# The last expert group of a mixture of experts summed in PSUM over all columns, and the combination that follows it reordered

## The chip, the cores and the metric

The kernel runs on one core of a Trainium2 chip. The metric is the device time of one execution in microseconds (us). Times of the kernel before are 2087.3, 2087.61 and 2090.02 us; their median is 2087.61 us.

## The reference, cut to what matters

The program is two transformer blocks on 512 tokens of D = 1024 columns. The first ends with a mixture of experts, the second begins with a normalisation and a product with a wide matrix:

```python
def expert_block(acc, blk):                 # blocks of rows sorted by expert
    tok, wts, e = blk
    out = swiglu(h_pad[tok], w_gu[e], w_down[e])
    return acc.at[tok].add(out * wts[:, None].astype(out.dtype)), None
...
f = acc[:N] + swiglu(h, w_sh_gu, w_sh_down)             # routed sum + shared expert
x = x_lat + gt2 * rms_norm(f, g_post_ffn)               # end of the first block
...
xn = rmsnorm(x, norm_mix_gain)                          # start of the second block
...                                                     # xn @ w_in, of which w_v is the first part used
```

So every token's row needs the sum of eight routed expert outputs and of one shared expert, two normalisations one after the other, and only then can the next product start.

## The kernel before, in words

Tokens lie in four tiles of 128 (NT = 4). All products are made in three passes: each factor is split into a rounded high part (ACT, L133 for weights, L153 for activations) and a low rest (DVE, L134 and L154), and TensorE adds hi·hi, lo·hi and hi·lo (`mm3`, L147 to L149).

**Expert groups.** Routed rows are worked off in groups of blocks. For a group, the loop in the function around L1297 to L1350 makes the expert's output rows `ey` (ACT, L1072), in a ring of three tiles. Columns 0 to 383 (CA = 384) of `ey` are split into `eys` hi (ACT, L1085) and lo (GpSimd, L1086), and TensorE adds them to the tokens' sums `acc[t]` in PSUM through a one-hot matrix `eoh` (`expert_add`, L1095). Columns 384 to 1023 go by an indirect DMA of GpSimd's software queue (`expert_send`, L1076) which adds them in DRAM, in two buffers `cb[0]` and `cb[1]`. The last group has one block of 96 rows.

**Shared expert.** After the groups comes a branch for overflow blocks, not taken here (L1356); all engines meet at it. Then `shared_out` adds the shared expert's product: per token tile six matmuls of 512 columns into `acc[t]` (columns 0 to 511), six into `mm` (columns 512 to 1023).

**Combination** (`second_block`, L1462 to L1535). SP loads, per token tile, the DRAM sums `cf<-cb` (L1462) and `cg<-cb` (L1463), and the rows `g`, `cx`, `gmix`. `take(t)` forms the whole sum in `cf`: ACT copies `acc`'s 384 columns (L1480), DVE (tile 0) or GpSimd (tiles 1 to 3) adds `cg` (L1481), DVE adds `acc`'s other 128 columns (L1482) and `mm` (L1483) straight from PSUM. ACT takes the sum of squares (L1486); `rstd` (L178 to L186) is eight small DVE operations for one tile, or eleven for tiles 1 to 3 at once. Then the product with the gain and the add to `cx` (tile 0: L714; later tiles `norm`: L1510 and the `add2` L1404, 640 columns on DVE, 384 on GpSimd), the second sum of squares (ACT, L1486 or L1388), a second `rstd`, and `xn` (L1498 or L1390). TensorE transposes `xn` (`tp`, L1398), ACT and DVE split the transposed tile into `x` hi and lo (L153, L154), and the product with w_v begins: two halves of 512 columns per tile, (0,0), (0,1), (1,0) and so on, 24 matmuls each, `tp` of the next tile after them or between them. w_v comes in four pieces of two units: v0 and v1 feed the first halves, v2 and v3 the second; v3's low parts are made by GpSimd (L134).

PSUM of the first block is given back by `release()`; only then can the second block's PSUM tiles (the transposes first of all) be used. The order on DVE, ACT and GpSimd inside the combination is the order in which it is written; TensorE's and SP's is set by a scheduler. The combination's tiles lie in SBUF that the expert part's tiles had used, so its first writers wait for the last readers of those.

Of the kernel before, what the change touches and what calls it, by code (L numbers as in the profile page):

```python
# [11 lines left out]
F = mybir.dt.float32  # L12
R = mybir.dt.float32r
# [3 lines left out]
AF = mybir.ActivationFunctionType  # L17
OP = mybir.AluOpType
# [6 lines left out]
D = 1024  # L25
# [41 lines left out]
class Kernel:  # L67
# [1009 lines left out]
                                          in_=y[p0:p1, CA:], in_offset=None, bounds_check=T - 1, oob_is_err=False,  # L1077
                                          compute_op=OP.add)

    def expert_parts(self, mp, y, row):  # L1080

        nc = self.nc
        m = row.shape[0]
        yh, yl = (mp.tile([128, CA], R, tag=f"eys{i}", name="eys", bufs=2)[0:m] for i in range(2))
        nc.scalar.activation(yh, y[0:m, :CA], AF.Copy)  # L1085
        last = nc.gpsimd.tensor_sub(yl, y[0:m, :CA], yh.bitcast(F))  # L1086
        oh = mp.tile([128, T], R, tag="eoh", name="eoh", bufs=2)[0:m]
        nc.vector.tensor_scalar(oh, self.route["iota"][0:m], row, None, op0=OP.is_equal)
        return (oh, (yh, yl)), last
# [7 lines left out]
    def shared_expert(self, mp, pp, gp, gT, h2T):  # L1097
# [4 lines left out]
        for h in range(2):  # L1102
            hs = slice(h * H, (h + 1) * H)
            sg = []
            for u in range(2):
                for j in range(2):
# [7 lines left out]
                        nc.vector.tensor_mul(sg[j], sg[j], ps[:, :H])  # L1114
                        self.split_ps(gT[0][:, j, hs], gT[1][:, j, hs], sg[j])
                    yield
    def shared_out(self, ps, gT, w, t, half):

        c = slice(half * 512, (half + 1) * 512)
        for i in range(2):  # L1120
            self.mm3(ps, [z[:, i, t * 128:(t + 1) * 128] for z in gT], [z[:, i, c] for z in w],
                     half == 1 and i == 0, i == 1)

    def first_block(self):

# [84 lines left out]
    def experts(self, mp, pp, h2d, cb, acc, shared, gT, sums, grow, ahead, extra):  # L1210
# [83 lines left out]
        nc.vector.tensor_scalar(zr, r["iota"], -1.0, None, op0=OP.is_equal)  # L1294
        for t in range(NT):
            nc.tensor.matmul(acc[t], zr[:, 0:128], zr, start=True, stop=False)
        late, sums = None, []  # L1297
        for g in range(len(groups) + 1):
            turn(g + 1)
            outs, now, y = [], None, []  # L1300

            def advance():

                if late:
                    lg, a, nums = late
                    aT = [self.expert_turn(more, pp, x) for x in a]
                    y.extend(mp.tile([128, D], F, tag="ey", name="ey", bufs=3) for _ in a)
                    for j, e in enumerate(nums):
                        outs.append((e, [(b, aT[b], tabs[rows_of[lg][b]][1], y[b], p0, p1)
                                         for b, parts in enumerate(groups[lg][1]) for i, p0, p1, _ in parts if i == j]))  # L1310

            def add():
                while sums:
                    self.expert_add(acc, *sums.pop(0))

            def finish():

                if not outs:
                    return
                e, parts = outs.pop(0)  # L1320
                lg = late[0]
                self.expert_out(pp, dn(e), [p[1:] for p in parts])
                last = None
                if not outs:
                    add()
                    for b, i in enumerate(rows_of[lg]):
                        s, last = self.expert_parts(mp, y[b], tabs[i][0])
                        sums.append(s)
                with tc.issue_after(last.ins) if last else ExitStack():
                    for b, _, _, y_, p0, p1 in parts:  # L1330
                        i = rows_of[lg][b]
                        gi = tabs[i][3][[p[1] for p in groups[lg][1][b]].index(p0)]
                        self.expert_send(y_, gi, p0, p1, next(sent))

            if g < len(groups):
                es, bs = groups[g]
                a = [mp.tile([128, 256], F, tag="eact", name="act", bufs=4)[0:b[-1][2]] for b in bs]
                now = g, a, []
                for j, e in enumerate(es):
                    e = number(e)  # L1340
                    now[2].append(e)
                    self.expert_in(mp, pp, gu(e), [(xT[g][b][i], a[b], p0, p1) for b, parts in enumerate(bs)
                                                   for i, (k, p0, p1, _) in enumerate(parts) if k == j],
                                   None if j else advance)
                    finish()
            else:
                advance()
            while outs:
                finish()
            late = now  # L1350
# [20 lines left out]

        rest = []
        for t in range(NT):
            self.shared_out(acc[t], gT, w, t, 0)
            rest.append(pp.tile([128, 512], F, tag="mm", name="mm", bufs=4))
            self.shared_out(rest[t], gT, w, t, 1)
        return rest


# [13 lines left out]
    def turn_tile(self, pp, xn, hi, lo, t):  # L1393
        ts = slice(t * 128, (t + 1) * 128)
        for u in range(2):
# [1 line left out]
            for i in range(4):  # L1397
                self.nc.tensor.transpose(ps[:, i], xn[:, (4 * u + i) * 128:(4 * u + i + 1) * 128], self.ident)  # L1398
            self.split_ps(hi[:, 4 * u:4 * u + 4, ts], lo[:, 4 * u:4 * u + 4, ts], ps)

    def add2(self, dst, a, b):

        for sl, e in ((slice(0, ADD_COLS), self.nc.vector), (slice(ADD_COLS, D), self.nc.gpsimd)):
            e.tensor_add(dst[:, sl], a[:, sl], b[:, sl])  # L1404

    def quarters(self, name, *at):

# [33 lines left out]
    def second_block(self, x1d, cb, acc, more, release):  # L1441
# [9 lines left out]
        vr = vctx.enter_context(right("b2v")).tile([128, NT, D], F, name="rv")  # L1451
        with right("comb") as wp, ExitStack() as wctx:
            fs = [wp.tile([128, D], F, name=f"cf{t}") for t in range(NT)]
            f2 = [wp.tile([128, D - CA], F, name=f"cg{t}") for t in range(NT)]

            sq, y = vr[:, 3], vr[:, 2]
            g3 = wp.tile([128, D], F, name="g3")
# [1 line left out]
            ss = wp.tile([128, NT], F, name="css")  # L1459
            rows = [slice(t * 128, (t + 1) * 128) for t in range(NT)]  # L1460
            def sums(t):
                nc.sync.dma_start(fs[t][:, CA:], cb[0][rows[t], :])  # L1462
                nc.sync.dma_start(f2[t], cb[1][rows[t], :])  # L1463

            sums(0)
# [4 lines left out]
                sums(t)  # L1470
            for t in range(1, NT):
                nc.sync.dma_start(x1[t], x1d[rows[t], :])
            units = self.each_unit(wctx, self.quarters("w_v_2"), self.first_raws, [None, None, None, nc.gpsimd])
            ET = mybir.EngineType
            with tc.manual_schedule(engines={ET.DVE, ET.Activation, ET.Pool}):
                w = [next(units), next(units)]

                def take(t):

                    nc.scalar.activation(fs[t][:, 0:CA], acc[t][:, 0:CA], AF.Copy)  # L1480
                    (nc.gpsimd if t else nc.vector).tensor_add(fs[t][:, CA:], fs[t][:, CA:], f2[t])  # L1481
                    nc.vector.tensor_add(fs[t][:, CA:512], fs[t][:, CA:512], acc[t][:, CA:])  # L1482
                    nc.vector.tensor_add(fs[t][:, 512:], fs[t][:, 512:], more[t])  # L1483

                def squares(x, ss):
                    nc.scalar.activation(sq, x, AF.Square, accum_out=ss)  # L1486


                take(0)
                squares(fs[0], ss[:, 0:1])  # L1490
                nc.vector.tensor_mul(y, fs[0], g3)
                self.scale_add(x1[0], y, self.rstd(wp, ss[:, 0:1], D), x1[0])
                ss0 = wp.tile([128, 1], F, name="css0")
                squares(x1[0], ss0)
                nc.vector.tensor_mul(y, x1[0], gain)
                take(1)
                xn = wp.tile([128, D], F, tag="xn", name="xn", bufs=2)
                nc.vector.tensor_scalar(xn, y, self.rstd(wp, ss0, D), None, op0=OP.mult)  # L1498
                for t in range(2, NT):
                    take(t)  # L1500
                for t in range(1, NT):
                    squares(fs[t], ss[:, t:t + 1])
                release()
                pp = ctx.enter_context(tc.tile_pool(name="b2ps", bufs=1, space=PSUM))
                rs = self.rstd(wp, ss[:, 1:], D)
                self.turn_tile(pp, xn, xs[0], xs[1], 0)
                nc.sync.dma_start(xd[rows[0], :], x1[0])

                def norm(t):
                    nc.vector.scalar_tensor_tensor(fs[t], fs[t], rs[:, t - 1:t], g3, op0=OP.mult, op1=OP.mult)  # L1510
                    self.add2(x1[t], x1[t], fs[t])
                    nc.sync.dma_start(xd[rows[t], :], x1[t])

                def product(t, half, between=None):
                    ps = self.tile_gemm(pp, self.columns(xs), w, half, t, between)
                    nc.scalar.activation(vr[:, t, half * 512:(half + 1) * 512], ps, AF.Copy)

                norm(1)
                w.append(next(units))
                xn = self.normed_tile(wp, x1[1], gain)  # L1520
                w.append(next(units))
                w = [w[:2], w[2:]]
                for t in range(NT):
                    product(t, 0)
                    if t + 2 < NT:
                        norm(t + 2)
                    turn = None
                    if t + 1 < NT:
                        turn = lambda: self.turn_tile(pp, xn, xs[0], xs[1], t + 1)
                    product(t, 1, turn)  # L1530
                    if t + 2 < NT:
                        xn = self.normed_tile(wp, x1[t + 2], gain)
# [409 lines left out]
RAW2 = 2  # L1942
MOD_SPLIT = (1, 2, 3)
RAW3 = 2
ADD_COLS = 640

CA = 384
AHEAD = 3
# [139 lines left out]
```

## Time and profile before

| | |
|---|---|
| runs | 2087.3, 2087.61, 2090.02 us; median 2087.61 us |
| the profiled execution's own time | 2089.45 us |
| its span on the core | 2087.7 us, so 1.75 us lie around the span |
| mean granted TensorE clock | 0.982 of full speed |
| TensorE busy | 1969.7 us (94% of the span) |
| DVE, ACT, GpSimd busy | 1524.8, 1156.2, 512.1 us |

The places that matter lie between 1255 and 1335 us after the span's start. PE is TensorE, DVE VectorE, ACT ScalarE, POOL GpSimd, SP the engine that issues most loads. A line number is one of the kernel before; where the changed kernel's own line is meant, the text says so.

### The profile page before, as it was taken

The numbers are of one execution on the slowest core, as the hardware profiler recorded it, in microseconds if no ns is written. First come the engines' busy times: TensorE is split into PE (matmuls) and PEld (weight loads), VectorE is DVE, ScalarE is ACT, GpSimd is POOL, SyncE is SP. The second block draws the span as 40 slices with busy tenths as digits, with TensorE's granted clock in tenths as the row PEclk, the third lists the DMA queues.
The fourth block names the chain that finished last, engine by engine and source line by source line (L and its number), as shares of the span: only waits on it lengthen the run. The fifth ranks groups of instructions, "written<-read, shape, count | busy, mean of one in ns | idle before, by whom it ended". The sixth has DMA issues, their size and how long they took to land. (4 is left out here: it accounts for less than half of the span.)

```text
span 2087.7 us, 27579 instructions
## 1 busy us (share of the span) xinstructions
PE 1969.7 (94%) x9935; PEld 1583.8 (76%) x9935; DVE 1524.8 (73%) x2689; ACT 1156.2 (55%) x1734; POOL 512.1 (25%) x291
## 2 busy tenths in 40 slices
PE   7999999999889999899999996999999999999997
PEld 4877888787877677667766775777788888888886
DVE  6667766657899899899999997456863345755657
ACT  6544433233368798788888885334232324554554
POOL 0322221101236465445634323111100000000000
PEclk9999999999899999999999998999999999999999
DMA  7201126543489999899998997411122234546553
GB/s 294 80 22 43 68 98 252 212 166 132 168 302 349 312 343 351 284 353 340 353 347 306 330 333 252 143 61 61 41 91 91 99 143 134 159 126 197 123 140 81
DMA packets 73167, 406.03 MB, mean 194 GB/s; under 512 B 11758, under 2 KB 12735, under 8 KB 31428
## 3 DMA queue, kind: packets, MB, share of 16 engines
q1 hardware_dynamic: 58084, 360.18, 46.7%
q0 software_dynamic: 14944, 44.06, 9.7%
q8 instruction: 79, 1.29, 0.2%
q14 instruction: 60, 0.49, 0.1%
HBM read 388.07 MB, written 24.86 MB: 198 GB/s over the span
## 5 line engine op out<-in xcount | busy, mean ns | idle before, releaser
L134 DVE TENSOR_TENSOR wlo<-raw,whi 128x1024 fp32r<-128x1024 f32 x610 | 745.7, 1249 | 176.2 <-ACT whi L133 171.5
L133 ACT ACTIVATE whi<-raw 128x1024 fp32r<-128x1024 f32 x616 | 631.0, 1055 | 291.6 <-PE mm L148 178.5
L1076 POOL DMA_INDIRECT cb<-ey,sgi x67 | 151.6, 2262 | 158.8 <-ACT ey L1072 139.7
L1086 POOL TENSOR_TENSOR eys<-ey,eys 128x384 fp32r<-128x384 f32 (+2 forms) x47 | 102.9, 2191 | 126.4 <-ACT eys L1085 126.2
L147 PE MATMUL mm<-hT,whi 128*128 128x512 f32 x320 | 127.1, 397 | 0.6 <-DVE yb L369 0.6
L148 PE MATMUL mm<-hT,whi 128*128 128x512 f32 x320 | 125.9, 394 | 0.0
L149 PE MATMUL mm<-hT,wlo 128*128 128x512 f32 x320 | 125.5, 392 | 0.0
L148 PE MATMUL mm<-x,whi 128*128 128x512 f32 x304 | 122.5, 403 | 0.0
L147 PE MATMUL mm<-x,whi 128*128 128x512 f32 x304 | 120.9, 398 | 0.0
L149 PE MATMUL mm<-x,wlo 128*128 128x512 f32 x304 | 120.9, 398 | 0.0
L1034 PE MATMUL mm<-wlo,xT 128*128 128x512 f32 (+1 forms) x280 | 114.4, 409 | 4.1 <-DVE wlo L134 3.9
L1034 PE MATMUL mm<-whi,xT 128*128 128x512 f32 (+1 forms) x280 | 113.1, 404 | 0.3 <-ACT ey L1072 0.3
L148 PE MATMUL mm<-wlo,eaT 128*128 128x512 f32 (+2 forms) x268 | 106.6, 399 | 1.1 <-DVE wlo L134 0.9
L147 PE MATMUL mm<-whi,xT 128*96 128x512 f32 (+1 forms) x256 | 105.5, 412 | 0.3 <-DVE esum L1047 0.3
L148 PE MATMUL mm<-wlo,xT 128*96 128x512 f32 (+1 forms) x256 | 102.7, 401 | 3.1 <-DVE wlo L134 3.1
L149 PE MATMUL mm<-whi,eaT 128*128 128x512 f32 (+2 forms) x268 | 105.1, 394 | 0.0
L147 PE MATMUL mm<-whi,eaT 128*128 128x512 f32 (+2 forms) x268 | 101.7, 396 | 3.3 <-ACT eaT L153 1.7
L982 POOL DMA_INDIRECT xg<-h2d,sgi x47 | 79.8, 1699 | 97.9 <-issue 28.9
L147 PE MATMUL mm<-y,whi 128*128 128x512 f32 (+2 forms) x272 | 103.2, 379 | 0.0
L149 PE MATMUL mm<-y,wlo 128*128 128x512 f32 (+2 forms) x272 | 103.1, 379 | 0.0
L148 PE MATMUL mm<-y,whi 128*128 128x512 f32 (+2 forms) x272 | 103.1, 379 | 0.0
L149 PE MATMUL mm<-whi,xT 128*96 128x512 f32 (+1 forms) x256 | 101.3, 396 | 0.0
(591 smaller groups left out, 4684.9 us busy)
## 6 DMA issues: line engine op xcount, KB each, us to landing
raw<-in_w_expert_gu SPq DMA_DIRECT2D x128, 1024.0 KB
raw<-in_w_expert_down SPq DMA_DIRECT2D x64, 1024.0 KB
raw<-in_w_in SPq DMA_DIRECT2D x41, 1024.0 KB
raw<-in_w_ff SPq DMA_DIRECT2D x32, 1024.0 KB
raw<-in_w_ada SPq DMA_DIRECT2D x24, 1024.0 KB
raw<-in_w_ff POOLq DMA_DIRECT2D x16, 1024.0 KB
raw<-in_w_out SPq DMA_DIRECT2D x8, 1024.0 KB
raw<-in_w_v SPq DMA_DIRECT2D x4, 1024.0 KB
```

The lines of the kernel that those rows point to most:

```text
L133: nc.scalar.activation(hi, rv[:, k:k + n], AF.Copy)
L134: (engine or nc.vector).tensor_sub(lo, rv[:, k:k + n], hi.bitcast(F))
L147: mm(ps, ah, bh, start=start, stop=False)
L148: mm(ps, ah, bl, start=False, stop=False)
L149: mm(ps, al, bh, start=False, stop=stop)
L982: self.nc.gpsimd.indirect_dma_start(out=xg[0:gi.shape[0]], out_offset=None, in_=h2d, in_offset=bass.IndirectOffsetOnAxis(ap=gi, axis=0), b ...
L1034: nc.tensor.matmul(ps[0:xT[0].shape[2]], xT[0][:, kk], z[:, k], start=kk == i == 0, stop=kk == KD - 1 and i == 1)
L1076: self.nc.gpsimd.indirect_dma_start(out=cb, out_offset=bass.IndirectOffsetOnAxis(ap=gi, axis=0), in_=y[p0:p1, CA:], in_offset=None, bounds ...
L1086: last = nc.gpsimd.tensor_sub(yl, y[0:m, :CA], yh.bitcast(F))
```

## The change

In the last group, if it has one block (it has), all 1024 columns of its output are split (`eyw` hi on ACT, lo on DVE, in two pieces of 512 columns, from the `ey` ring), its indirect DMA is left out, and its sums are added in the last loop: two matmuls of 512 columns (hi and lo) ahead of the six shared ones, for each token tile and half. In the combination, ACT copies all 1024 columns of every tile out of PSUM, and PSUM is released right after; the DRAM sums of a tile are added to each other and to the copy by DVE, for tiles 1 to 3 only in `norm(t)`; `rstd` is taken tile by tile; GpSimd does nothing; the piece v2 of w_v is split inside `norm(1)`, v3's low part is made by DVE.

```diff
-    def expert_parts(self, mp, y, row):
+    def expert_parts(self, mp, y, row, whole=False):
...
+        if whole:
+            yh, yl = (mp.tile([128, D], R, tag="ey", name="eyw", bufs=3)[0:m] for _ in range(2))
+            for c in range(0, D, 512):
+                sl = slice(c, c + 512)
+                nc.scalar.activation(yh[:, sl], y[0:m, sl], AF.Copy)
+                last = nc.vector.tensor_sub(yl[:, sl], y[0:m, sl], yh[:, sl].bitcast(F))
+        else:
...
+        whole = lambda g: g == len(groups) - 1 and len(groups[g][1]) == 1
...
-                        sums.append(s)
+                        (ends if whole(lg) else sums).append(s)
+                if whole(lg):
+                    return
...
-            self.shared_out(acc[t], gT, w, t, 0)
             rest.append(pp.tile([128, 512], F, tag="mm", name="mm", bufs=4))
-            self.shared_out(rest[t], gT, w, t, 1)
+            for half, ps in enumerate((acc[t], rest[t])):
+                for n, (oh, ys) in enumerate(ends):
+                    for i, y in enumerate(ys):
+                        nc.tensor.matmul(ps, oh[:, t * 128:(t + 1) * 128], y[:, half * 512:(half + 1) * 512],
+                                         start=half == 1 and n == i == 0, stop=False)
+                self.shared_out(ps, gT, w, t, half, half == 1 and not ends)
...
-            units = self.each_unit(wctx, self.quarters("w_v_2"), self.first_raws, [None, None, None, nc.gpsimd])
+            units = self.each_unit(wctx, self.quarters("w_v_2"), self.first_raws)
...
-                    nc.scalar.activation(fs[t][:, 0:CA], acc[t][:, 0:CA], AF.Copy)
-                    (nc.gpsimd if t else nc.vector).tensor_add(fs[t][:, CA:], fs[t][:, CA:], f2[t])
-                    nc.vector.tensor_add(fs[t][:, CA:512], fs[t][:, CA:512], acc[t][:, CA:])
-                    nc.vector.tensor_add(fs[t][:, 512:], fs[t][:, 512:], more[t])
+                    nc.scalar.activation(fs[t][:, 0:512], acc[t], AF.Copy)
+                    nc.scalar.activation(fs[t][:, 512:], more[t], AF.Copy)
+
+                def add(t):
+
+                    nc.vector.tensor_add(f1[t], f1[t], f2[t])
+                    nc.vector.tensor_add(fs[t][:, CA:], fs[t][:, CA:], f1[t])
...
                 take(0)
+                add(0)
                 squares(fs[0], ss[:, 0:1])
+                for t in range(1, NT):
+                    take(t)
+                release()
+                pp = ctx.enter_context(tc.tile_pool(name="b2ps", bufs=1, space=PSUM))
...
-                def norm(t):
-                    nc.vector.scalar_tensor_tensor(fs[t], fs[t], rs[:, t - 1:t], g3, op0=OP.mult, op1=OP.mult)
-                    self.add2(x1[t], x1[t], fs[t])
+                def norm(t, between=None):
+                    add(t)
+                    squares(fs[t], ss[:, t:t + 1])
+                    if between:
+                        between()
+                    rs = self.rstd(wp, ss[:, t:t + 1], D)
+                    nc.vector.scalar_tensor_tensor(fs[t], fs[t], rs, g3, op0=OP.mult, op1=OP.mult)
+                    nc.vector.tensor_add(x1[t], x1[t], fs[t])
```

On PE, at the end of the shared expert's product, the last half of the last token tile stood before so (`shT` is the shared expert's activation, `tp` the transposes of the combination's first tile):

```order
L147 MATMUL mm<-whi,shT_4000 128x512
L148 MATMUL mm<-wlo,shT_4000 128x512
L149 MATMUL mm<-whi,shT_4001 128x512
L147 MATMUL mm<-whi,shT_4000 128x512
L148 MATMUL mm<-wlo,shT_4000 128x512
L149 MATMUL mm<-whi,shT_4001 128x512
L1398 MATMUL tp<-ident,xn 128x128 x8
```

and stands now so (L1388 and L1412 are lines of the changed kernel):

```order
L1388 MATMUL mm<-eyw,eoh 128x512 x2
L147 MATMUL mm<-whi,shT_4000 128x512
L148 MATMUL mm<-wlo,shT_4000 128x512
L149 MATMUL mm<-whi,shT_4001 128x512
L147 MATMUL mm<-whi,shT_4000 128x512
L148 MATMUL mm<-wlo,shT_4000 128x512
L149 MATMUL mm<-whi,shT_4001 128x512
L1412 MATMUL tp<-ident,xn 128x128 x8
```

The same pair stands ahead of each of the eight groups of six, so `eyw` and `eoh` are read until six matmuls before the end. SP's first load of the combination (now L1471), ACT's first copy (L1489) and DVE's first add (L1494) write tiles that lie where `eyw` and `eoh` lie, and each of them waits in the built program for the last of these L1388 matmuls.

On SP, at the start of the combination, the change has (lines of the changed kernel; `cg` now holds both DRAM sums):

```order
L119 DMA raw<-in_w_v 128x2048
L119 DMA raw<-in_w_in 128x2048
L1471 DMA cg_13595<-cb_93 128x640
L1472 DMA cg_13599<-cb_94 128x640
L1475 DMA g_13603<-g3d 128x1024
L1476 DMA cx_13604<-x1d 128x1024
```

The load of w_in stood behind the combination's loads before; it is now ahead of them, and behind the first of them stand `g`, `cx` and `gmix`, as before.

On ACT, the combination's first part stood before so:

```order
L1480 ACTIVATE cf_13584<-acc_5221 128x384
L1486 ACTIVATE rv,css<-cf_13584 128x1024
L1486 ACTIVATE rv,css_13652<-cx_13593 128x1024
L1480 ACTIVATE cf_13585<-acc_5222 128x384
L1480 ACTIVATE cf_13586<-acc_5223 128x384
L1480 ACTIVATE cf_13587<-acc_5224 128x384
```

and stands now so:

```order
L1489 ACTIVATE cf_13591<-acc_5221 128x512
L1490 ACTIVATE cf_13591<-mm 128x512
L1498 ACTIVATE rv,css<-cf_13591 128x1024
L1489 ACTIVATE cf_13592<-acc_5222 128x512
L1490 ACTIVATE cf_13592<-mm 128x512
L1489 ACTIVATE cf_13593<-acc_5223 128x512
L1490 ACTIVATE cf_13593<-mm 128x512
L1489 ACTIVATE cf_13594<-acc_5224 128x512
L1490 ACTIVATE cf_13594<-mm 128x512
L1498 ACTIVATE rv,css_13674<-cx_13604 128x1024
L153 ACTIVATE x_13582<-tp 128x4x128 x2
```

The six copies of tiles 1 to 3 stand between the squares of tile 0's two normalisations (L1498), and so behind a wait for DVE's adds of tile 0. DVE has between tile 1's `xn` and the low part of tile 1's transposed rows (L154), where two instructions stood before, now the whole of `norm(2)`: two adds of 640 columns, an `rstd` of eight that waits for ACT's squares, the product with the gain and an add of 1024 columns.

## Rows read from the trace of the kernel before

**Rows 1.** The page: engines' busy time, and the chain that ended last.

```profile
PE 1969.7 (94%) x9935; PEld 1583.8 (76%) x9935; DVE 1524.8 (73%) x2689; ACT 1156.2 (55%) x1734; POOL 512.1 (25%) x291
...
PE 32%; DVE 4%; issue 1%; ACT 1%; DMA 0%; POOL 0%; ACTq 0%; DVEq 0%
```

**Rows 2.** Timeline of PE: start, duration (us), what, count, idle before it.

```profile
1263.45 2.83 PE L1095 MATMUL acc<-eys,eoh 128*128 128x384 f32 x14
...
1268.98 0.47 PE L147 MATMUL mm<-whi,shT 128*128 128x512 f32 x1 [0.88 <-DVEq L1356]
...
1278.62 0.39 PE L149 MATMUL mm<-whi,shT 128*128 128x512 f32 x1
1291.78 1.94 PE L1398 MATMUL tp<-ident,xn 128*128 128x128 f32 x8 [12.77 <-DMA xd<-cx]
...
1308.96 1.27 PE L1398 MATMUL tp<-ident,xn 128*128 128x128 f32 x8 [2.83 <-DVE xn L1390]
...
1322.39 1.03 PE L1398 MATMUL tp<-ident,xn 128*128 128x128 f32 x8
```

**Rows 3.** Timeline of SP's queue: start, duration of the issue, what, count.

```profile
1271.10 0.33 SPq L1462 DMA_DIRECT2D cf<-cb  x1
1271.47 0.42 SPq L1463 DMA_DIRECT2D cg<-cb  x1
```

**Rows 4.** Timeline of DVE, same columns.

```profile
1268.92 1.22 DVE L134 TENSOR_TENSOR wlo<-raw,whi 128x1024 fp32r<-128x1024 f32 x1 [0.44 <-DVEq L1356]
1276.76 0.82 DVE L1481 TENSOR_TENSOR cf<-cf,cg 128x640 f32<-128x640 f32 x1 [6.62 <-DMA cg<-cb]
...
1278.61 1.23 DVE L1491 TENSOR_TENSOR rv<-cf,g 128x1024 f32<-128x1024 f32 x1
1279.85 0.15 DVE L178 TENSOR_SCALAR rsx<-css 128x1 f32<-128x1 f32 x1
...
1281.57 1.28 DVE L714 SCALAR_TENSOR_TENSOR cx<-rv,rsy,cx 128x1024 f32<-128x1024 f32 x1
1282.89 2.50 DVE L1495 TENSOR_TENSOR rv<-cx,gmix 128x1024 f32<-128x1024 f32 x1
1285.31 0.27 DVE L1482 TENSOR_TENSOR cf<-cf,acc 128x128 f32<-128x128 f32 x1
...
1286.11 0.14 DVE L178 TENSOR_SCALAR rsx<-css 128x1 f32<-128x1 f32 x1
...
1289.23 0.75 DVE L1498 TENSOR_SCALAR xn<-rv,rsy 128x1024 f32<-128x1024 f32 x1
...
1290.89 0.68 DVE L1483 TENSOR_TENSOR cf<-cf,mm 128x512 f32<-128x512 f32 x1
...
1302.05 2.12 DVE L182 SCALAR_TENSOR_TENSOR rsz<-rsy,rsx 128x1 f32<-128x1 f32 x1
...
1307.53 1.28 DVE L1390 SCALAR_TENSOR_TENSOR xn<-cx,rsy,gmix 128x1024 f32<-128x1024 f32 x1
...
1310.79 1.28 DVE L154 TENSOR_TENSOR x<-tp,x 128x512 fp32r<-128x512 f32 x2
```

**Rows 5.** Timeline of ACT, same columns.

```profile
1262.32 0.67 ACT L1072 ACTIVATE ey<-mm,swt 96x512 f32<-96x512 f32 x1
...
1278.66 1.06 ACT L1486 ACTIVATE rv<-cf 128x1024 f32<-128x1024 f32 x1 [7.00 <-DVE cf L1483]
...
1300.63 2.00 ACT L133 ACTIVATE whi<-raw 128x1024 fp32r<-128x1024 f32 x2
1302.99 0.60 ACT L1516 ACTIVATE rv<-mm 128x512 f32<-128x512 f32 x1 [0.36 <-PE mm L149]
```

**Rows 6.** Timeline of POOL, same columns.

```profile
1282.77 5.50 POOL L1481 TENSOR_TENSOR cf<-cf,cg 128x640 f32<-128x640 f32 x3 [15.63 <-DMA cf<-cb]
...
1301.76 4.76 POOL L134 TENSOR_TENSOR wlo<-raw,whi 128x1024 fp32r<-128x1024 f32 x2 [2.21 <-ACT whi L133]
```

**Rows 7.** Stretches (us): length, busy of PE, PEld, DVE, ACT, POOL, PEclk, DMA share, GB/s.

```profile
1268.00:1279.00 11.00, 10.12 (x43) 7.81 (x42) 3.80 (x6) 0.83 (x2) 0.00 (x0) 1.00 0.95 315
1279.00:1291.70 12.70, 0.01 (x1) 0.00 (x0) 11.96 (x26) 5.06 (x10) 5.41 (x3) 0.63 1.01 401
1291.70:1299.30 7.60, 7.11 (x19) 4.89 (x20) 5.62 (x16) 4.46 (x8) 1.34 (x1) 0.50 0.03 14
...
1309.00:1313.00 4.00, 4.00 (x15) 3.34 (x16) 3.03 (x4) 1.19 (x2) 1.59 (x1) 0.59 0.52 217
```

More of the change, by code (lines that the diff above doesn't have):

```diff
@@ L1078, in expert_send @@
                                           compute_op=OP.add)
-    def expert_parts(self, mp, y, row):
+    def expert_parts(self, mp, y, row, whole=False):
         nc = self.nc
         m = row.shape[0]
-        yh, yl = (mp.tile([128, CA], R, tag=f"eys{i}", name="eys", bufs=2)[0:m] for i in range(2))
-        nc.scalar.activation(yh, y[0:m, :CA], AF.Copy)
-        last = nc.gpsimd.tensor_sub(yl, y[0:m, :CA], yh.bitcast(F))
+        if whole:
[5 more added lines that the diff above has]
+        else:
+            yh, yl = (mp.tile([128, CA], R, tag=f"eys{i}", name="eys", bufs=2)[0:m] for i in range(2))
+            nc.scalar.activation(yh, y[0:m, :CA], AF.Copy)
+            last = nc.gpsimd.tensor_sub(yl, y[0:m, :CA], yh.bitcast(F))
         oh = mp.tile([128, T], R, tag="eoh", name="eoh", bufs=2)[0:m]
@@ L1116, in shared_expert, with shared_out @@
                     yield
-    def shared_out(self, ps, gT, w, t, half):
+    def shared_out(self, ps, gT, w, t, half, start):
         c = slice(half * 512, (half + 1) * 512)
         for i in range(2):
-            self.mm3(ps, [z[:, i, t * 128:(t + 1) * 128] for z in gT], [z[:, i, c] for z in w],
-                     half == 1 and i == 0, i == 1)
+            self.mm3(ps, [z[:, i, t * 128:(t + 1) * 128] for z in gT], [z[:, i, c] for z in w], start and i == 0, i == 1)
     def first_block(self):
@@ L1296, in experts @@
             nc.tensor.matmul(acc[t], zr[:, 0:128], zr, start=True, stop=False)
-        late, sums = None, []
+        late, sums, ends = None, [], []
+        whole = lambda g: g == len(groups) - 1 and len(groups[g][1]) == 1
         for g in range(len(groups) + 1):
@@ L1326, in finish @@
                     for b, i in enumerate(rows_of[lg]):
-                        s, last = self.expert_parts(mp, y[b], tabs[i][0])
-                        sums.append(s)
+                        s, last = self.expert_parts(mp, y[b], tabs[i][0], whole(lg))
+                        (ends if whole(lg) else sums).append(s)
+                if whole(lg):
+                    return
                 with tc.issue_after(last.ins) if last else ExitStack():
@@ L1399, in turn_tile @@
             self.split_ps(hi[:, 4 * u:4 * u + 4, ts], lo[:, 4 * u:4 * u + 4, ts], ps)
-    def add2(self, dst, a, b):
-        for sl, e in ((slice(0, ADD_COLS), self.nc.vector), (slice(ADD_COLS, D), self.nc.gpsimd)):
-            e.tensor_add(dst[:, sl], a[:, sl], b[:, sl])
     def quarters(self, name, *at):
@@ L1453, in second_block @@
             fs = [wp.tile([128, D], F, name=f"cf{t}") for t in range(NT)]
-            f2 = [wp.tile([128, D - CA], F, name=f"cg{t}") for t in range(NT)]
+            f1, f2 = ([wp.tile([128, D - CA], F, name=f"cg{i}{t}") for t in range(NT)] for i in range(2))
             sq, y = vr[:, 3], vr[:, 2]
@@ L1461, in sums @@
             def sums(t):
-                nc.sync.dma_start(fs[t][:, CA:], cb[0][rows[t], :])
+                nc.sync.dma_start(f1[t], cb[0][rows[t], :])
                 nc.sync.dma_start(f2[t], cb[1][rows[t], :])
@@ L1495, in second_block @@
                 nc.vector.tensor_mul(y, x1[0], gain)
-                take(1)
                 xn = wp.tile([128, D], F, tag="xn", name="xn", bufs=2)
                 nc.vector.tensor_scalar(xn, y, self.rstd(wp, ss0, D), None, op0=OP.mult)
[L1499 to L1505, printed above, removed]
                 self.turn_tile(pp, xn, xs[0], xs[1], 0)
                 nc.sync.dma_start(xd[rows[0], :], x1[0])
-                def norm(t):
-                    nc.vector.scalar_tensor_tensor(fs[t], fs[t], rs[:, t - 1:t], g3, op0=OP.mult, op1=OP.mult)
-                    self.add2(x1[t], x1[t], fs[t])
+                def norm(t, between=None):
[6 more added lines that the diff above has]
+                    nc.vector.tensor_add(x1[t], x1[t], fs[t])
                     nc.sync.dma_start(xd[rows[t], :], x1[t])
@@ L1516, in product @@
                     nc.scalar.activation(vr[:, t, half * 512:(half + 1) * 512], ps, AF.Copy)
-                norm(1)
+                norm(1, lambda: w.append(next(units)))
                 w.append(next(units))
                 xn = self.normed_tile(wp, x1[1], gain)
-                w.append(next(units))
                 w = [w[:2], w[2:]]
@@ L1944 @@
 RAW3 = 2
-ADD_COLS = 640
 CA = 384
```

## The prediction

> **What bounds the kernel now.** The page comes first: TensorE is busy for 94% of the span and is by far the largest share of the chain that ended last [rows 1], so a change of some microseconds is read where TensorE stands still. The timeline of PE gives those places [rows 2]. The shared expert's last 42 matmuls run from 1268.98 to 1279.01, at 9.64 / 41 = 0.235 us each. Then PE is idle for 12.77 us until the first transpose, tp(0), at 1291.78; it stands again for 2.83 us ahead of tp(1), at 1308.96; tp(2), at 1322.39, follows its forerunner without idle time, and from there PE has work. Whatever tp(2) loses or gains is, as I read it, what the end loses or gains.
>
> Next, who fills the 12.77 us. SP issues the loads of the DRAM sums at 1271.10 and 1271.47 [rows 3]; DVE's first add begins at 1276.76, after 6.62 us of idleness that a DMA ended [rows 4]. So the loads are issued while PE still computes. From the first add to the end of xn (1289.23 + 0.75) are 13.22 us of DVE and ACT. tp(0) comes 1.8 us later still: the row names a DMA, but what ends at the right time is DVE's last add out of PSUM, 1290.89 + 0.68 = 1291.57, which gives PSUM back [rows 2, 4]. The clock is the last view: it falls within the idle stretch (0.63 granted on average) and is 0.50, the 1.2 GHz level, until 1299.3; after the gap ahead of tp(1) it falls again (0.59 from 1309 to 1313) [rows 7]. A gap thus costs its length and some slow matmuls behind it.
>
> **The last group.** Removed from PE: 8 adds of 384 columns, some 0.2 us each (14 took 2.83) [rows 2]; they lay ahead of the branch. Added: 16 of 512 columns at 0.235, of which the first two precede the row at 1268.98; 14 x 0.235 = 3.3 us lie behind it. Their inputs: ACT's two hi pieces cost about 0.67 each as the ey row of that shape, in place of one eys copy [rows 5]; DVE's two lo pieces about 0.65 each (x lo: 1.28 for two [rows 4]), ahead of the branch at which PE waited 0.88 us for DVE [rows 2]. One wlo of 1.22 [rows 4] moves behind the branch in exchange, but DVE's first lo starts later than the wlo it displaces, since it needs the new hi and the ring's buffer. I take +1.1 us for the branch, between 0 and 2. PE's end: 1279.0 + 1.1 + 3.3 = 1283.4. The indirect DMA left out saves SP a wait, which is worth nothing here, as the next step shows.
>
> **The new wait.** The loads' tiles lie over eyw and eoh, and the last reader of these is the L1388 pair of the last half tile, six matmuls before PE's end. That pair is done near 1281.9. SP's first load, issued before at 1271.10, waits for it: +10.8 us. Behind it on SP's queue stand the second load, g, cx, gmix and the loads of tiles 1 to 3; who waits for them is DVE's first add. From issue to that add were 5.66 us [rows 3, 4], with the same five loads sharing the DMA engines; I keep 5.66, which puts the add at 1287.6. If the engines gave 401 GB/s (1279 to 1291.7) in place of 315 [rows 7], it would be 5.66 x 315 / 401 = 4.4, 1.2 less. The load of w_in that is moved ahead is issued near 1271 and long done; it costs nothing.
>
> **From the first add to tp(0).** The old 13.22 us lose: the product with gmix takes 2.50 beside POOL's adds [rows 4, 6] where one of the same shape takes 1.23, 1.27 less; the second rstd takes 3.12 (1286.11 to 1289.23) where the first takes 1.72 (1279.85 to 1281.57), 1.40 less; tile 1's two PSUM adds, 0.80 (1285.31 to 1286.11); tile 0's two are replaced by one of 640 columns, 0.1 less [rows 4]. They gain 0.55: the squares of cx stand on ACT behind squares of 1.06 and six copies of 0.60 [rows 5], a little longer than DVE's rstd and L714. That is 10.2, so tp(0) at 1297.8, **+6.0 us**. PSUM is free by then (the copies end near 1294), so the 1.8 us for it are in this gain.
>
> Here the Trainium skill speaks for the change. First the row: the 2.50 us lie inside POOL's 5.50 us of adds, the instruction being slower by 1.27 [rows 4, 6]. SBUF — State Buffer, section "Who interferes with whom", says that VectorE and GpSimd share a port pair and that a VectorE instruction with two SBUF inputs is blocked by a GpSimd instruction that reads SBUF; by that rule alone all such stretches go and tp(0) would come earlier, not later. The trace agrees in kind. The first rival below is that outcome.
>
> **From tp(0) to tp(1).** DVE's order is now x lo(0), add(1), low parts of v2, rstd, product, add, low parts of v3, rstd, xn, each step's price from [rows 4, 5]: x lo starts 1.8 after tp(0) as it did after tp(1) (1308.96, 1310.79), 1299.6; its two halves end at 1300.9; two adds of 0.82 give 1302.5; ACT's squares 1.2 (1.06 and a short read of the sum), then hi of v2 at 1.0 each; so low v2 ends at 1307.1; rstd 1.72, product 1.28, add 1.23: 1311.3; low v3 2.4: 1313.7; rstd 1.72, xn 1.28: 1316.7. Before, xn ended at 1308.81, though three POOL operations had slowed DVE (L182 took 2.12 beside POOL's wlo [rows 4, 6]). tp(1) comes at 1316.8, **+7.8 us**.
>
> **From tp(1) to tp(2).** x lo(1) now stands behind norm(2): two adds 1.64 (1318.3), squares 1.2, rstd 1.72 (1321.3), 1.28 and 1.23 (1323.8), first low half 0.64: 1324.4. Before, it began at 1310.79, two microseconds behind tp(1) [rows 2, 4]. x hi(1) also waits on ACT behind the squares of tile 2. PE makes four matmuls of tile 1, then stands some three microseconds. The 36 matmuls left until tp(2) cost 0.235 each, 8.5, plus 1.6 for slow ones as after the gap ahead of 1309 (4.0 us at 0.59) [rows 7]: tp(2) at 1334.5, **+12.1 us**. By the same prices the low half of tile 2 comes about when its first matmul could use it, and nothing further is late.
>
> **The sum** against the profiled execution: span 2087.7 + 12.1 + 1.75 around it = 2101.55; that execution lay 1.84 over the median, so I predict 2099.7 us for the median. A measurement of this kernel tells about 0.2%, 4.2 us, from no change.
>
> **Rivals.** *Faster:* the loads are not held, because the memory they write is free earlier than I read. Then the first add stays near 1277, and 10.2 us later, at 1287.2, tp(0) could start; that is 4.6 us earlier than 1291.78 and gives 2083.0, the outcome of the port rule too. It decides if the loads are issued before about 1275.8, that is 1271.10 plus the 4.7 us that the shorter chain and the freed PSUM give. For it: POOL's stretches and the 1.8 us are real. Against it: the wait stands in the built program, and its matmul is six before the end. 0.06. *No change:* loads land in 4.4, the branch costs 0, and tile 1's waits are hidden because the gaps shrink; I get +6.0 - 1.2 - 1.1 = +3.7, 2091.3. Against it: norm(2)'s queue ahead of x lo(1) is there whatever the loads do. 0.07. *Slower by more:* PE's clock, at 0.50 for 7.6 us of work after the first gap [rows 7], stays there through tile 1 after three gaps in a row; 36 matmuls at twice 0.235 cost 8.5 more, less the 1.6 counted: +19.0, 2106.6. Against it: after one gap of 2.83 us the half level lasted only until 1313. 0.16. That the change does nothing is excluded by its order on PE.
>
> **How the numbers follow.** My case has 0.71. Within it the branch (-1.1 to +0.9), the landing (-1.2), the copies and the stall at tile 1 (3 either way) are open, 2094.5 to 2103.5. To hold 8 in 10 I reach to the slow-clock case and leave out most of the two quick ones: 2093.5 to 2107. Faster by over 0.2%: 0.06; within: 0.07; slower: 0.87.
>
> **What would show it.** Right: SP's first load of the sums near 1282 and DVE's first add near 1287.6; tp(0) near 1298, tp(1) near 1317, tp(2) near 1334.5; DVE's product with gmix at about 1.25; a stall of PE ahead of tile 1's first matmuls with x lo. Wrong: loads issued near 1271, or x lo(1) within 3 us of tp(1), or a clock of 0.50 well into tile 1's second half.

## The result, and the profile after

The changed kernel takes 2098.57 us (median; 2097.2 to 2102.1), against 2087.45 us for the kernel before beside it. The ratio is 1.0053, with a 95% interval of 1.0037 to 1.0069: slower by about 11 us. 2099.7 was forecast, with a range of 2093.5 to 2107. The profiled execution took 2098.03 us with a span of 2096.3 us.

The two traces differ by half a microsecond before the place of the change, so times are compared from a common mark, the last expert group's first transposes (`tp<-ident,act`), which start at 1258.36 before and 1257.88 after. First the timeline of PE of the changed kernel (start, duration in us, what, count, idle time before it and what ended it), beside [rows 2]:

```profile
1257.88 0.33 PE L1057 MATMUL tp<-ident,act 96*128 96x96 f32 x2
...
1265.95 0.50 PE L1388 MATMUL acc<-eyw,eoh 96*128 96x512 f32 x1 [1.14 <-DVE eyw L1089]
1268.98 0.70 PE L1388 MATMUL mm<-eyw,eoh 96*128 96x512 f32 x2 [1.13 <-DVEq L1366]
...
1280.22 0.62 PE L1388 MATMUL mm<-eyw,eoh 96*128 96x512 f32 x2
...
1295.62 1.94 PE L1412 MATMUL tp<-ident,xn 128*128 128x128 f32 x8 [13.38 <-issue]
...
1310.47 0.80 PE L148 MATMUL mm<-wlo,x 128*128 128x512 f32 x1 [3.43 <-DVE wlo L134]
...
1315.33 1.34 PE L1412 MATMUL tp<-ident,xn 128*128 128x128 f32 x8
1317.85 0.50 PE L147 MATMUL mm<-whi,x 128*128 128x512 f32 x1 [1.18 <-ACT x L153]
...
1322.26 0.50 PE L149 MATMUL mm<-whi,x 128*128 128x512 f32 x1 [3.22 <-DVE x L154]
...
1331.94 1.03 PE L1412 MATMUL tp<-ident,xn 128*128 128x128 f32 x8
```

The last pair on `eyw` starts at 1280.22. The timeline of SP's queue, beside [rows 3], shows what waited for it:

```profile
1271.37 0.33 SPq L119 DMA_DIRECT2D raw<-in_w_in  x1
1280.97 0.33 SPq L1471 DMA_DIRECT2D cg<-cb  x1
1281.35 0.43 SPq L1472 DMA_DIRECT2D cg<-cb  x1
```

The first load of the sums is issued 0.75 us after that pair's start, 0.13 us after its end. The view of waits names the same pair, for SP's queue and for ACT's first copy (us in total, times, longest):

```profile
SPq L1471 <- PE mm L1388: 8.7, 1, 8.7
ACT cf L1489 <- PE mm L1388: 12.8, 1, 12.8
```

The timeline of DVE, beside [rows 4]:

```profile
1285.32 0.82 DVE L1494 TENSOR_TENSOR cg<-cg,cg 128x640 f32<-128x640 f32 x1 [13.97 <-DMA cg<-cb]
...
1287.52 1.23 DVE L1508 TENSOR_TENSOR rv<-cf,g 128x1024 f32<-128x1024 f32 x1 [0.45 <-DMA g<-g3d]
...
1291.70 1.22 DVE L1512 TENSOR_TENSOR rv<-cx,gmix 128x1024 f32<-128x1024 f32 x1
...
1294.66 0.75 DVE L1514 TENSOR_SCALAR xn<-rv,rsy 128x1024 f32<-128x1024 f32 x1
...
1313.18 1.28 DVE L1404 SCALAR_TENSOR_TENSOR xn<-cx,rsy,gmix 128x1024 f32<-128x1024 f32 x1
1314.38 0.82 DVE L1494 TENSOR_TENSOR cg<-cg,cg 128x640 f32<-128x640 f32 x1
...
1321.52 1.28 DVE L154 TENSOR_TENSOR x<-tp,x 128x512 fp32r<-128x512 f32 x2
```

The reader is to see three things. DVE's idle time ahead of its first add has grown from 6.62 to 13.97 us. The product with `gmix` takes 1.22 us, with GpSimd silent, instead of 2.50. And x lo(1), which began 1.8 us behind tp(1), now begins 6.2 us behind it, since `norm(2)` (from 1314.38) is ahead of it.

From the common mark, in us:

| | loads issued | first add | tp(0) | tp(1) | tp(2) | tp(3) |
|---|---|---|---|---|---|---|
| before | 12.74 | 18.40 | 33.42 | 50.60 | 64.03 | 75.80 |
| after | 23.09 | 27.44 | 37.74 | 57.45 | 74.06 | 86.19 |
| later by | 10.35 | 9.04 | 4.32 | 6.85 | 10.03 | 10.39 |

tp(3)'s shift of 10.4 us is close to the 11 us by which the times differ. (The spans of the two profiled executions differ by 8.6 us only; single executions of one kernel scatter by some microseconds, as the ranges above show.) The clock's share in the shift is seen in stretches of the changed kernel (length, busy us of PE, PEld, DVE, ACT and POOL, granted clock, DMA share, GB/s):

```profile
1295.60:1299.00 3.40, 3.38 (x12) 2.79 (x13) 1.46 (x3) 1.19 (x2) 0.00 (x0) 0.52 0.97 395
1299.00:1303.00 4.00, 4.00 (x20) 3.29 (x19) 1.74 (x3) 2.40 (x4) 0.00 (x0) 1.00 0.12 47
...
1310.00:1315.30 5.30, 4.83 (x11) 3.69 (x12) 4.99 (x13) 0.94 (x3) 0.00 (x0) 0.50 0.71 271
...
1322.20:1327.00 4.80, 4.74 (x14) 3.74 (x15) 4.46 (x13) 0.59 (x2) 0.00 (x0) 0.64 0.27 109
1327.00:1332.00 5.00, 5.00 (x24) 4.08 (x23) 1.40 (x7) 1.63 (x3) 0.00 (x0) 1.00 0.00 0
```

After each of the three gaps (13.38, 3.43 and 3.22 us) PE works at 0.50 to 0.64 for some 3 to 5 us and is back at 1.00 by 1327, well ahead of tile 1's end.

### The profile page after: what moved, and what is told of

Same layout as the page of the kernel before. It is cut to its first block, busy times and chain, and to the rows that moved or that the text cites. A ratio compares the mean times of both kernels' runs of the same rounds, so it can differ in the third digit from the quotient of the medians.

```text
span 2096.3 us, 27586 instructions
## 1 busy us (share of the span) xinstructions
PE 1974.5 (94%) x9943; PEld 1586.0 (76%) x9943; DVE 1527.8 (73%) x2705; ACT 1159.1 (55%) x1739; POOL 492.4 (23%) x281
```

## The experiments

Two suspects were open: the hold (loads, copies and first add wait for the last reader of `eyw` and `eoh`), which comes with the last group, and the order on DVE and ACT, which comes with the combination. All ratios are against the kernel before, run on the same chip beside the experiment.

**1. The adds made first.** All 16 adds of the last group stand ahead of the 48 shared matmuls.

```diff
+        rest = [pp.tile([128, 512], F, tag="mm", name="mm", bufs=4) for t in range(NT)]
+        for half in range(2):
+            for t in range(NT):
+                ps = (acc, rest)[half][t]
...
         for t in range(NT):
             for half, ps in enumerate((acc[t], rest[t])):
                 self.shared_out(ps, gT, w, t, half, half == 1 and not ends)
```

> The changed kernel with the 16 adds of the last group all made ahead of the 48 shared matmuls, so that the last reader of eyw and eoh is done some 10 us earlier; nothing else is changed. Theory (the hold: the combination's loads, copies and adds wait for the last reader of eyw and eoh, whose memory they take): SP's first load of the sums is issued near 1272 instead of 1281, tp(0) comes about 8 us earlier than in the changed kernel (near 1287.5), and all later transposes with it: about 2090 us. Rival (the loss is made in the combination, by its order on DVE and ACT, and the late loads would be hidden by the product anyway): the loads go early, but tp(2) moves by under 2 us: about 2097 us.

2091.33 us (2089.55 to 2096.09), ratio 1.0014 (1.0003 to 1.0025): about 3 us slower than before. In PE's timeline the adds now end near 1270.6:

```profile
1255.75 0.33 PE L1057 MATMUL tp<-ident,act 96*128 96x96 f32 x2
...
1266.82 3.75 PE L1388 MATMUL mm<-eyw,eoh 96*128 96x512 f32 x8 [1.03 <-DVEq L1366]
...
1287.09 1.94 PE L1414 MATMUL tp<-ident,xn 128*128 128x128 f32 x8 [4.50 <-issue]
```

and SP's first load follows at once:

```profile
1270.70 0.33 SPq L1473 DMA_DIRECT2D cg<-cb  x1
```

From the mark, tp(0) comes at 31.34 and tp(3) at 79.51, 6.4 and 6.7 us earlier than in the changed kernel, with nothing done to the combination. The hold costs that much, and it is carried to the end: the rival, which gave tp(2) under 2 us, falls, since tp(2) moves by 6.7. The expectation of 8 us for tp(0) was too large, because the loads took longer from issue to the first add (6.44 us against 4.35). What is left of the loss lies behind tp(0): tp(0) is 2.1 us earlier than in the kernel before and tp(3) 3.7 us later. That is the new combination's order, which runs 2 and 4 look at.

**2. The low part first.** In the changed kernel `norm(2)` and `norm(3)` are written behind the split of the transposed tile.

```diff
                     product(t, 0)
-                    if t + 2 < NT:
-                        norm(t + 2)
...
                     product(t, 1, turn)
                     if t + 2 < NT:
+                        norm(t + 2)
                         xn = self.normed_tile(wp, x1[t + 2], gain)
```

> The changed kernel with norm(2) and norm(3) written behind the split of the transposed tile, so that x lo(1) and x lo(2) stand ahead of them on DVE; nothing else is changed. Theory (order on DVE costs a stall of 3.2 us ahead of tile 1's matmuls with x lo, and 1.2 ahead of x hi): both stalls go, but xn(2) comes later by the same operations, near 1329.7, so that tp(2) comes 2 us earlier than in the changed kernel: about 2096.5 us; between 2094.5 and 2098.5. Rival (only the hold matters): no change, 2098.5 us. Rival (norm(2) is then the late one): tp(2) waits for xn(2) and is later, 2100 us or more.

2095.72 us (2094.22 to 2100.28), ratio 1.0034 (1.0021 to 1.0047), some 3 to 4 us less than the changed kernel's 1.0053; the two intervals overlap, so that the times alone do not tell the two kernels apart. The PE timeline:

```profile
1255.74 0.33 PE L1057 MATMUL tp<-ident,act 96*128 96x96 f32 x2
...
1312.70 1.07 PE L1412 MATMUL tp<-ident,xn 128*128 128x128 f32 x8 [1.36 <-DVE xn L1404]
1314.02 0.50 PE L147 MATMUL mm<-whi,x 128*128 128x512 f32 x1 [0.25 <-ACT x L153]
...
1326.79 1.07 PE L1412 MATMUL tp<-ident,xn 128*128 128x128 f32 x8 [1.58 <-DVE xn L1404]
...
1340.89 1.07 PE L1412 MATMUL tp<-ident,xn 128*128 128x128 f32 x8 [1.61 <-DVE xn L1404]
```

Both stalls behind tp(1) are gone, and a shorter one, for xn(2), stands ahead of tp(2): 14.09 us from tp(1) to tp(2) instead of 16.61. tp(2) comes 3.0 us earlier from the mark. The theory's mechanism and its new wait are both there. But most of it does not last: the same wait, now for xn(3), stands ahead of tp(3), and the step from tp(2) to tp(3) takes 14.10 us instead of 12.13. At tp(3) the run is 1.0 us earlier than the changed kernel. So the trace shows what the order does within tile 1, and rules out that xn(2) comes later than the stall it replaces; a gain of 3 to 4 us for the whole it does not show.

**3. The new last group alone**, with the combination of before.

```diff
-            f1, f2 = ([wp.tile([128, D - CA], F, name=f"cg{i}{t}") for t in range(NT)] for i in range(2))
+            f2 = [wp.tile([128, D - CA], F, name=f"cg{t}") for t in range(NT)]
...
```

> The new last group with the combination of before. Theory (the hold belongs to the last group): the loads are issued near 1281.5, tp(0) comes near 1301, as the old combination's longer chain and its PSUM wait stay, tp(1) 17.2 us later as before; about 2098 us, within 2 us of the changed kernel. Rival (the combination makes the loss): within 3 us of the kernel before, 2087.5 to 2090.5 us.

2098.11 us (2093.26 to 2099.84), ratio 1.0043 (1.0026 to 1.006). The old combination, with its longer chain, starts from the same late loads:

```profile
1254.91 0.33 PE L1057 MATMUL tp<-ident,act 96*128 96x96 f32 x2
...
1298.15 1.94 PE L1412 MATMUL tp<-ident,xn 128*128 128x128 f32 x8 [19.08 <-issue]
...
1315.37 1.07 PE L1412 MATMUL tp<-ident,xn 128*128 128x128 f32 x8 [2.52 <-DVE xn L1404]
```

PE is idle for 19.08 us; tp(0) is 9.8 us later than before, tp(3) 8.3. The last group alone makes most of the loss, and the rival, which had it within 3 us of the kernel before, falls.

**4. The new combination alone**, with the last group of before.

```diff
-        whole = lambda g: g == len(groups) - 1 and len(groups[g][1]) == 1
+        whole = lambda g: False
```

> The old last group with the new combination. Theory: the loads are issued near 1271.1 as before; from the first add to xn it takes 10.1 us instead of 13.2, and PSUM is free, so tp(0) comes about 5 us earlier than before, near 1286.7; from tp(0) to tp(1) it takes 2.5 us more than before and from tp(1) to tp(2) 3.2 more, which gives nearly all of it back: about 2088 us, between 2086 and 2090. Rival (the combination makes the loss): over 2094 us. Rival (GpSimd's share was all that held DVE back): tp(0) and all later ones 5 us earlier, about 2082.5 us.

2089.89 us (2088.57 to 2093.59), ratio 1.0007 (0.9997 to 1.0016): no difference that this measurement tells. But it is no idle change. Its PE timeline:

```profile
1257.22 0.33 PE L1057 MATMUL tp<-ident,act 96*128 96x96 f32 x2
...
1286.60 1.94 PE L1412 MATMUL tp<-ident,xn 128*128 128x128 f32 x8 [8.64 <-issue]
...
1301.45 0.80 PE L148 MATMUL mm<-wlo,x 128*128 128x512 f32 x1 [3.12 <-DVE wlo L134]
...
1308.83 0.50 PE L147 MATMUL mm<-whi,x 128*128 128x512 f32 x1 [2.16 <-ACT x L153]
...
1313.24 0.80 PE L149 MATMUL mm<-whi,x 128*128 128x512 f32 x1 [3.23 <-DVE x L154]
```

tp(0) comes 4.0 us earlier than before; three stalls of 3.12, 2.16 and 3.23 us behind it give that and 2.9 us more back by tp(3). Both rivals fall: the combination alone does not make the loss of 11 us, and the early tp(0) does not survive.

**5. The combination alone with the low part first**: the edits of 2 and 4 together.

> The old last group, the new combination, and norm(2) and norm(3) behind the split of the transposed tile. Theory (with the loads not held, the order on DVE is all that is left of the loss): tp(0) and tp(1) as in the combination alone, 4.0 and 2.2 us earlier than before; from tp(1) to tp(2) 14.1 us as in the run with x lo first, instead of 18.1, so tp(2) about 1.5 us earlier than before: 1 to 3 us faster than the kernel before. Rival (the stall at x lo is hidden by later waits): as the combination alone, 0 to 2 us slower than before.

2088.31 us (2084.35 to 2092.02), ratio 0.9995 (0.9985 to 1.0004): 1 us faster in the middle, and not to be told from no change. The PE timeline:

```profile
1262.23 0.33 PE L1057 MATMUL tp<-ident,act 96*128 96x96 f32 x2
...
1310.45 1.07 PE L1412 MATMUL tp<-ident,xn 128*128 128x128 f32 x8
...
1324.54 1.07 PE L1412 MATMUL tp<-ident,xn 128*128 128x128 f32 x8 [1.58 <-DVE xn L1404]
...
1338.62 1.06 PE L1412 MATMUL tp<-ident,xn 128*128 128x128 f32 x8
```

The times from the mark are tp(1) 48.22 and tp(3) 76.39, where the combination alone has 48.39 and 78.71. The step from tp(1) to tp(2) is 14.09 us, as expected, and tp(2) is 1.7 us earlier than before. But as in run 2 the next step is longer, 14.08 us against 11.77 before, so that tp(3) is 0.6 us later than before. The expected 1 to 3 us for the whole kernel are not shown.

**6. The combination reordered.** The old last group; three pieces of w_v split in DVE's and ACT's idle time ahead of the first add; the tiles' sums added and squared earlier, so that `norm(2)` ahead of x lo(1) keeps only its rstd, product and add.

```diff
-                w = [next(units), next(units)]
+                w = [next(units) for _ in range(3)]
...
+                add(1)
                 self.turn_tile(pp, xn, xs[0], xs[1], 0)
...
-                def norm(t, between=None):
-                    add(t)
-                    squares(fs[t], ss[:, t:t + 1])
-                    if between:
-                        between()
+                def norm(t):
...
-                norm(1, lambda: w.append(next(units)))
+                squares(fs[1], ss[:, 1:2])
+                add(2)
+                norm(1)
+                squares(fs[2], ss[:, 2:3])
                 w.append(next(units))
...
                         xn = self.normed_tile(wp, x1[t + 2], gain)
+                    if t + 3 < NT:
+                        add(t + 3)
+                        squares(fs[t + 3], ss[:, t + 3:t + 4])
```

> The old last group and the new combination in another order: three of the four pieces of w_v are split ahead of the first add, where DVE and ACT stand still; the sums of tile 1 are added between xn(0) and x lo(0), those of tile 2 right behind, those of tile 3 behind xn(2), each with its squares; x lo(1) stands behind the product and add of norm(2). Theory (the chain on DVE from tp(0) to tp(2) is what gives the early tp(0) back): from tp(0) to tp(1) 16.7 us, TensorE's own work at the lower clock, from tp(1) to tp(2) 12 us; tp(2) 5 us earlier than before and the kernel 3 to 6 us faster than before. Rival (an earlier tp(0) only lets TensorE run its first matmuls at the lower clock for longer, and the time is lost there): no faster than the run with x lo first, 1 to 3 us faster than before.

2081.74 us (2079.02 to 2084.55), ratio 0.9964 (0.9952 to 0.9976): 7.5 us faster than before by the ratio, better than both kernels and than the 3 to 6 us expected. The PE timeline:

```profile
1258.44 0.33 PE L1057 MATMUL tp<-ident,act 96*128 96x96 f32 x2
...
1285.71 1.94 PE L1412 MATMUL tp<-ident,xn 128*128 128x128 f32 x8 [6.66 <-issue]
...
1300.12 1.07 PE L1412 MATMUL tp<-ident,xn 128*128 128x128 f32 x8 [0.75 <-DVE rsx L178]
1301.43 0.50 PE L147 MATMUL mm<-whi,x 128*128 128x512 f32 x1 [0.25 <-ACT x L153]
...
1304.80 0.50 PE L149 MATMUL mm<-whi,x 128*128 128x512 f32 x1 [2.15 <-DVE x L154]
...
1314.49 1.03 PE L1412 MATMUL tp<-ident,xn 128*128 128x128 f32 x8
```

tp(1) follows tp(0) after 14.41 us, less than the 16.7 put for PE's own work at the lower clock. Its stretches:

```profile
1285.70:1290.00 4.30, 4.29 (x16) 3.51 (x17) 3.70 (x6) 2.23 (x4) 0.00 (x0) 0.62 1.04 426
1290.00:1294.00 4.00, 4.00 (x20) 3.29 (x19) 3.69 (x11) 3.05 (x4) 0.00 (x0) 1.00 0.45 187
1294.00:1300.10 6.10, 5.37 (x24) 4.14 (x23) 5.79 (x14) 1.64 (x3) 0.00 (x0) 1.00 0.71 250
```

Of the first 4.3 us behind tp(0) only a part is at the lower clock, where the kernel before worked at 0.50 for 7.6 us [rows 7]. So the rival falls: the early tp(0) is not lost to the clock. The step from tp(1) to tp(2) missed its 12 us: it is 14.37, since PE still stands 2.15 us for x lo(1), behind what is left of `norm(2)`. From the mark, tp(0) stands at 27.27, tp(1) at 41.68 and tp(3) at 67.84, 8.0 us earlier than before and 10.9 earlier than in run 4. Of these 10.9 us, 2.2 were there at the first add already (17.28 against 19.44 from the mark), from loads that were issued and used sooner though SP's order is the same in both, so that this part cannot be put down to the reordering. Which of the changes made together here is worth how much was not tried.

**7. Both**: the reordered combination on the new last group with its adds made first (the edit of 1, and the order of 6).

> The same order of the combination with the new last group, its adds made ahead of the shared matmuls. Theory (the new last group costs TensorE 8 adds of 512 columns net and a wait at the branch, and the loads come 2 us later): tp(0) 2 us later than in the reordered combination with the old last group, and so 1 to 3 us slower than that run. Rival (the DMA left out is worth something once the loads are not held): as fast or faster than that run.

2083.26 us (2079.33 to 2087.64), ratio 0.9975 (0.9966 to 0.9984): 5.2 us faster than before, and by the ratios 2.3 slower than run 6 (0.9964), though the intervals overlap:

```profile
1255.96 0.33 PE L1057 MATMUL tp<-ident,act 96*128 96x96 f32 x2
...
1287.26 1.94 PE L1414 MATMUL tp<-ident,xn 128*128 128x128 f32 x8 [7.23 <-issue]
...
1301.92 1.04 PE L1414 MATMUL tp<-ident,xn 128*128 128x128 f32 x8
```

In the trace tp(0) comes 4.0 us later than in run 6 (31.30 from the mark against 27.27), and so does tp(3) (71.84 against 67.84): the theory's direction, at twice its size. Of the 4.0 us, 1.45 come from the loads' issue (14.12 from the mark against 12.67) and 2.6 from their way to the first add (7.24 us against 4.61). The rival, that the DMA left out is worth something once nothing is held, has nothing for it in the trace.

## Why the prediction was right

**What bounds the kernel, and the new wait.** Right. The loads were forecast to wait for the last L1388 pair and to be issued 10.8 us later; they were 10.35 later, and run 1 shows the cause by moving the reader alone: the loads then go 8.1 us earlier than in the changed kernel (14.95 from the mark against 23.09), and 6.7 us of that arrive at tp(3). In the changed kernel and in runs 1, 2 and 3 alike the first load is issued 0.13 us after the end of the last L1388 matmuls, wherever these stand. Run 3 shows the other half: the late loads come with the last group, whatever the combination. What these runs do not show is why the wait is there. That it is the memory of `eyw` and `eoh`, handed on to the combination's tiles, is read from the built program, in which the first load, copy and add each wait for that pair. To lay the two tiles into memory of their own was not tried.

**The last group on PE.** PE's last shared matmul starts 3.7 us later from the mark (23.97 against 20.26), where 4.4 had been summed; the branch cost 0.5 us (1268.98 - 1257.88 = 11.10 against 10.62) and not 1.1.

**The mis-sized term: the loads' way.** From the first load's issue to the first add 5.66 us were kept; it took 4.35 (1280.97 to 1285.32), a little under the low bound of 4.4. With the loads issued 0.45 us sooner than summed, the first add was so 9.0 and not 10.8 us late. The 5.66 had been taken from a stretch in which a w_v load and the last scatter came shortly before, but that does not explain it: with the same loads and scatter ahead, runs 4, 5 and 6 took 6.06, 4.32 and 4.61 us. The longest ways, 6.44 and 7.24 us, are those of runs 1 and 7, where the 1 MB load of w_in had been issued 1.49 and 0.94 us ahead; in runs 2 and 3, where it lay long behind, it was 4.03 and 4.80. No run isolates the cause, and it stays open.

**From the first add to tp(0).** 10.2 us were summed and 10.30 measured (1285.32 to 1295.62). Two small terms changed places, which is luck: ACT's copies did not hold the squares of `cx`, which had been put at 0.55, but the product with `g` waited 0.45 for its load. GpSimd's silence is seen in two rows: the product with `gmix` takes 1.22 us without GpSimd at work, against 2.50 beside it [rows 4], and the second rstd 1.72 (1292.94 to 1294.66 by the starts of its first operation and of xn) against 3.12. The Trainium skill, SBUF — State Buffer, "Who interferes with whom", says that a VectorE instruction with two SBUF inputs contends with a GpSimd instruction that reads SBUF. The trace agrees for the product with `gmix`, which has two such inputs. In run 4, where nothing is held, the way from the first add to tp(0) falls from 15.02 to 9.94 us; these two rows make 2.7 of the 5.1, and the rest is work on DVE and PSUM that moved. The rule was right about the chain and decided nothing about the whole, as the loads were held.

**From tp(0) to tp(2).** 19.0 and 17.7 us were summed for the two steps; 19.71 and 16.61 came out. The stall ahead of the matmuls with x lo was put at some three microseconds and is 3.22, and x hi waits 1.18 behind tile 2's squares. The path of the first step was not the one summed, though. The sum let tp(1) wait for xn(1), and DVE's chain up to there was right to 0.1 us (18.84 behind tp(0), 18.9 summed). But tp(1) did not wait for it: xn(1) was done at 1314.46, and PE came to tp(1) only at 1315.33, without standing still, because it had stood 3.43 us for v3's low part and then worked at the lower clock. This wait, on the same chain of DVE, was not named. Runs 2, 4 and 5 show that the order is the cause of the second step's length: with x lo first, the step from tp(1) to tp(2) falls from 16.6 to 14.1 us held, and from 18.1 to 14.1 not held. They also show that tp(2) does not stand for the end, as the prediction took it: in runs 2 and 5 the step behind it grows by some 2 us.

**The rivals.** *Faster* needed loads issued before about 1275.8; they came at 1280.97. *No change* needed the gaps behind tp(0) to shrink; they grew. *The clock held at its lower level through tile 1*: from 1322.2 to 1327 it was at 0.64 and then at 1.00, so that the case's 7 us did not come.

**The sum.** tp(2) was forecast 12.1 us later and is 10.0. The loads' way makes 1.3 us of the difference and their earlier issue 0.45; the two steps behind tp(0) missed by +0.7 and -1.1 and nearly cancel. The forecast of 12.1 for the whole stands against 11.1: the wait and the order were foreseen, and that the sum came so close owes something to errors of both signs.

## What to carry to other kernels

When work is moved to the end of a stage, look for its last reader, and for what stands in line behind that reader: here sixteen matmuls, cheap by themselves, held SP's next loads and ACT's copies for ten microseconds and DVE's first add for nine; by the built program, because the next stage's tiles lie in the memory that they read. An order written out by hand is worth reading as a chain for each consumer: what TensorE needs next (x lo, the low part of v3) stood behind work for the tile after it. And an engine's idle time ahead of a long chain is the cheapest place for work that the chain would otherwise carry: the run that split three pieces of weights there and added sums a step earlier (the two were not tried apart) was the fastest of all.

## What the runs showed that was not expected

The half of the clock after a gap lasted very differently long. Behind the 12.77 us gap of the kernel before, PE worked at 0.50 for 7.6 us [rows 7]; behind 13.38 us in the changed kernel it was at 0.52 for 3.4 us and then at 1.00. By the length of its matmuls, 0.63 us at the lower level and 0.39 at the full one, it was there for 3.3 us behind tp(0) in run 6, 5.8 in run 7 and 8.6 in run 3. In the kernel before and in run 3, which have the old combination and the longest stretches, PE stood once more for 0.3 us behind tp(0), for ACT's high part of a weight; in the others it did not, and still the stretches differ. No run was made to settle the cause, and it stays open. It matters little here: run 7, with its longer stretch, needs 14.66 us from tp(0) to tp(1), and run 6 14.41.
